# Entering the feed-forward layer: norms on VectorE alone, four gated products between the two halves, weight loads in quarters

## The chip, the cores and the metric

The kernel runs on one NeuronCore of a Trainium2 chip. The engines named below are TensorE (PE, with its weight loads as PEld), VectorE (DVE), ScalarE (ACT), GpSimd (POOL) and SyncE (SP), whose queue issues all DMA transfers of this kernel. Each engine works through its own instructions in a fixed order and waits where an operand or a buffer isn't there yet. The metric is the device time of one execution in microseconds (us).

## The reference

A decoder trunk of two layers, in float32, on 1024 tokens of width 1024. In both layers a mixer is followed by a projection, and that by a gated feed-forward layer (SwiGLU) of width 2816. The part that the change touches, cut from the reference:

```python
def rms_norm(x, g):
    y = x * lax.rsqrt(jnp.mean(x * x, axis=-1, keepdims=True) + EPS)
    return y * g
...
    mixed = jnp.concatenate([y, m_out], axis=-1) @ w_out[l]
    h = h + rms_norm(mixed, norm_mix_post[l])
    gu = rms_norm(h, norm_ffn_pre[l]) @ w_in          # 1024 x 5632
    g, u = gu[..., :D_FF], gu[..., D_FF:]
    f = (jax.nn.silu(g) * u) @ w_out_ffn
    h = h + rms_norm(f, norm_ffn_post[l])
```

Between the projection (`mixed`) and the feed-forward layer stand two norms, one after the other: the first of the projection's output, the second of the sum with the residual.

## The kernel before

Activations lie transposed: eight tiles of 128 features x 512 tokens for each half of the tokens (`H` = 512), held in float32. Each float32 operand of a matmul is split into a high part of type float32r and a low part that is the rest. `split` (L86) makes the high part with a copy on ScalarE (L87) and the low one with a subtraction on VectorE (L88). A product takes three matmuls: high by low, high by high, low by high. Names ending in h and l (`wh`, `wl`, `ah`, `al`, `ch`, `cl`, `th`, `tl`) are such parts; `ah` and `al` are those of the activations.

**The projection** (`mix_half`, L474) makes eight blocks of 24 matmuls (`mm<-al,wh`, L147 to L149) for each half. Layer 0 loads each block's weights (512 KB) for each half anew and splits them: the subtraction is on GpSimd in the first half and on VectorE in the second. In layer 1 the halves lie split in DRAM (`parted`), and `fetch` loads both (`wh` and `wl`, 512 KB each).

**The two norms** (`finish` in `mix_out`, L492). The sum of squares over the features is made with ones as the weights of a matmul (`rcol`, the `oo<-ones,...` rows of L227); `rcp` or `rcn` gets its scale and epsilon on VectorE (L231) and its power -1/2 on GpSimd (L232); a matmul with the identity spreads it over the partitions (`spread`, `oo<-ident,...` of L239), and ScalarE copies that to `rsp` for the first norm and `rsn` (or a tile tagged `hd`) for the second. `post` (L519) multiplies by `rsp` (L524, five of eight tiles on GpSimd), then multiplies by the gain and adds the residual (L526, VectorE), and stores the sum (`hx`). `sums` (L205) adds up the squares for the second norm on two tiles, one for each engine (L217). `scaled` (L534) multiplies by gain and `rsn`: four tiles in one instruction on VectorE (L540), four (`POOL_COPIES`) with a copy on ScalarE (L531) and a product on GpSimd (L538). Then each tile is split into `ah` and `al`.

**The order at the entry.** The first half's norms are worked through during the second half's projection. The second half's norms stand behind that projection. Meanwhile PE works on the first half of feed-forward blocks 0 and 1 (`ffn_plain`, L564: 96 matmuls of L574 to L576), and after these the same blocks for the second half, another 96. The order on each engine is set when the kernel is built, by a scheduler that goes by priorities (`WEIGHT_LEAD`, `EVICT_LEAD`, `NORM_LEAD`) and a simulated time line. `place` (L721) forces the four groups of matmuls of the second half's norms (two `rcol`, two `spread`) in between: the group of index i stands before the plain matmul whose number is `F_PLACES[i]`.

**The other 20 blocks** of 128 of the 2816 hidden features are made in pairs with seven products instead of eight (`ffn_block`, L624): sums and differences of quarters of the weight blocks (`combos`, L600) and of the activations (L742 to L747), 12 matmuls a product (L595 to L597), in the order 1, 5, 6, 2, 7, 3, 4. For each block SP loads the gate's and the up-projection's weights (`wraw`, 512 KB each, three buffers). GpSimd makes the sum `x` of two quarters of the second load (L613) and the other differences (L616, L618, L620), ScalarE and VectorE split them into `ch` and `cl`. Products 1 and 2 need no sums, and only the first half's activations. `out_weights` (L650) loads the output weights (`wo`), combines them and stores them (`wz`) for the last phase; `hidden_combos` stores the hidden features (`xz`).

## Time and profile before

| | |
|---|---|
| median of 3 runs | 2121.84 us (2115.52 to 2125.18) |
| profiled execution | 2116.97 us, of which the span is 2115.1 us |
| mean granted clock of TensorE | 0.974 |
| busy: TensorE, VectorE, ScalarE, GpSimd | 1999.0, 1444.4, 1042.2, 648.9 us |
| layer 0: second half's projection, then entry | 314.6 to 364.5 us, then to 446.2 us |
| layer 1: second half's projection, then entry | 1365.0 to 1405.8 us, from 1419.2 to 1498.2 us |

The span runs from the first to the last instruction of the profiled execution; 1.9 us of its time lie outside. In groups and timelines an instruction is named by its line, engine and operation, then output and inputs by the program's names with shapes, then how many; `[10.19 <-DVE al L88]` means that the engine was idle for 10.19 us before and that VectorE's instruction of line 88, which made `al`, ended that. Matmuls overlap, so PE's pace is read from one start to the next and not from the duration of one.

### The profile page before, as it was taken

The numbers are of one execution on the slowest core, as the hardware profiler recorded it, in microseconds if no ns is written. First come the engines' busy times: TensorE is split into PE (matmuls) and PEld (weight loads), VectorE is DVE, ScalarE is ACT, GpSimd is POOL, SyncE is SP. The second block draws the span as 40 slices with busy tenths as digits, with TensorE's granted clock in tenths as the row PEclk, the third lists the DMA queues.
The fourth block names the chain that finished last, engine by engine and source line by source line (L and its number), as shares of the span: only waits on it lengthen the run. The fifth ranks groups of instructions, "written<-read, shape, count | busy, mean of one in ns | idle before, by whom it ended". The sixth has DMA issues, their size and how long they took to land.

```text
span 2115.1 us, 27580 instructions
## 1 busy us (share of the span) xinstructions
PE 1999.0 (95%) x9400; PEld 1650.8 (78%) x9400; DVE 1444.4 (68%) x2218; ACT 1042.2 (49%) x1977; POOL 648.9 (31%) x575
## 2 busy tenths in 40 slices
PE   7999998799999999999999999887999999999997
PEld 6787776588877787888788878766888888878876
DVE  7877758777767667455878776777765665664566
ACT  6767775344443444444545576643433333344541
POOL 4333543723443431000035431346232233210012
PEclk9999999899999999999999999988999999999998
DMA  5422226137667679666545314152345444485653
GB/s 168 153 80 83 87 80 219 50 122 250 228 225 249 245 255 351 229 207 192 185 177 189 123 58 158 63 197 80 117 157 179 141 159 158 172 285 191 214 176 138
DMA packets 156766, 359.08 MB, mean 170 GB/s; under 512 B 17232, under 2 KB 22608, under 8 KB 156624
## 3 DMA queue, kind: packets, MB, share of 16 engines
q1 hardware_dynamic: 156624, 357.31, 49.2%
q8 instruction: 74, 1.21, 0.2%
q14 instruction: 68, 0.56, 0.1%
HBM read 255.53 MB, written 101.71 MB: 169 GB/s over the span
## 4 chain that ended last, share of the span: by engine, by line
PE 68%; DVE 12%; issue 8%; ACT 6%; POOL 4%; DMA 2%; SPq 0%; DVEq 0%; POOLq 0%; ACTq 0%
PE mm L595 10%; PE mm L597 10%; PE mm L596 9%; PE mm L697 6%; PE mm L698 6%; PE mm L699 6%; PE mm L149 4%; PE mm L147 4%; PE mm L148 4%; DVE acc L526 1%; PE mm L574 1%; PE mm L576 1%; PE mm L575 1%; DVE cl L88 1%; PE oo L1049 1%
## 5 line engine op out<-in xcount | busy, mean ns | idle before, releaser
L87 ACT CAST ch<-wraw 128x512 fp32r<-128x512 f32 x323 | 200.0, 621 | 389.7 <-PE mm L596 199.5
L88 DVE TENSOR_TENSOR cl<-wraw,ch 128x512 fp32r<-128x512 f32 x323 | 234.6, 727 | 188.9 <-ACT ch L87 186.2
L147 PE MATMUL mm<-al,wh 128*128 128x512 f32 x616 | 249.5, 405 | 13.4 <-DVE al L921 8.1
L149 PE MATMUL mm<-ah,wl 128*128 128x512 f32 x616 | 247.9, 403 | 7.0 <-DVE wl L88 5.0
L595 PE MATMUL mm<-al,ch 128*128 128x512 f32 x640 | 252.5, 395 | 1.5 <-DVE c L630 0.8
L597 PE MATMUL mm<-ah,cl 128*128 128x512 f32 x640 | 250.1, 395 | 3.5 <-DVE cl L88 3.5
L596 PE MATMUL mm<-ah,ch 128*128 128x512 f32 x640 | 250.6, 392 | 0.0
L148 PE MATMUL mm<-ah,wh 128*128 128x512 f32 x616 | 246.6, 400 | 0.0
L697 PE MATMUL mm<-tl,ch 128*128 128x512 f32 x532 | 208.1, 391 | 2.2 <-ACT ah L789 2.2
L699 PE MATMUL mm<-th,cl 128*128 128x512 f32 x532 | 206.8, 393 | 1.9 <-DVE cl L88 1.9
L698 PE MATMUL mm<-th,ch 128*128 128x512 f32 x532 | 207.7, 390 | 0.0
L595 PE MATMUL mm<-tl,ch 128*128 128x512 f32 x480 | 189.4, 395 | 1.7 <-ACT c L634 1.6
L596 PE MATMUL mm<-th,ch 128*128 128x512 f32 x480 | 187.8, 391 | 0.0
L597 PE MATMUL mm<-th,cl 128*128 128x512 f32 x480 | 185.4, 391 | 0.0
L613 POOL TENSOR_TENSOR x<-wraw 128x512 f32<-128x512 f32 x40 | 53.1, 1328 | 385.4 <-DMA wraw<-in_wi_dram 374.6
L147 PEld LDWEIGHTS mm<-al,wh 128*128 128x128 f32 x616 | 118.0, 192 | 41.6 <-DVE al L921 10.1
L597 PEld LDWEIGHTS mm<-ah,cl 128*128 128x128 f32 x640 | 120.4, 188 | 34.6 <-DVE cl L88 7.4
L149 PEld LDWEIGHTS mm<-ah,wl 128*128 128x128 f32 x616 | 118.1, 192 | 35.5 <-DVE wl L88 8.1
L595 PEld LDWEIGHTS mm<-al,ch 128*128 128x128 f32 x640 | 120.5, 188 | 28.4 <-ACT ch L87 1.9
L596 PEld LDWEIGHTS mm<-ah,ch 128*128 128x128 f32 x640 | 120.4, 188 | 27.2
L148 PEld LDWEIGHTS mm<-ah,wh 128*128 128x128 f32 x616 | 118.2, 192 | 23.1
L232 POOL TENSOR_TENSOR rcp<-rcp,mhalf 128x4 f32<-128x4 f32 x7 | 7.5, 1072 | 406.8 <-DVE rcp L231 406.8
(349 smaller groups left out, 4602.9 us busy)
## 6 DMA issues: line engine op xcount, KB each, us to landing
wraw<-in_wi_dram SPq DMA_DIRECT2D x88, 512.0 KB, 5.9
xz<-hd SPq DMA_DIRECT2D x154, 256.0 KB, 4.3
th<-xz SPq DMA_DIRECT2D x154, 256.0 KB, 3.5
wo<-in_wf_dram SPq DMA_DIRECT2D x44, 512.0 KB, 5.5
wz<-wo SPq DMA_DIRECT2D x44, 512.0 KB, 3.2
wraw<-wz SPq DMA_DIRECT2D x56, 256.0 KB, 3.3
wraw<-in_wa_dram SPq DMA_DIRECT2D x27, 512.0 KB, 3.5
wraw<-in_wf_dram SPq DMA_DIRECT2D x42, 256.0 KB, 3.5
```

The costliest lines, as they stand in the source:

```text
L87: self.nc.scalar.copy(hi, src)
L88: return (eng or self.nc.vector).tensor_tensor(lo, src, hi.bitcast(F32), op=ALU.subtract)
L147: self.mms += [nc.tensor.matmul(out, wh, al, start=i == 0, stop=False), nc.tensor.matmul(out, wh, ah, start=False, stop=False), nc.tensor. ...
L148: nc.tensor.matmul(out, wh, ah, start=False, stop=False),
L149: nc.tensor.matmul(out, wl, ah, start=False, stop=i == len(ks) - 1)]
L595: ins += [mm(out, wh, xl, start=start and k == 0, stop=False, skip_group_check=not start), mm(out, wh, xh, start=False, stop=False, skip_g ...
L596: mm(out, wh, xh, start=False, stop=False, skip_group_check=not start),
L597: mm(out, wl, xh, start=False, stop=k == 3, skip_group_check=not start)]
L613: ins = nc.gpsimd.tensor_tensor(x, a21, a22, op=ALU.add)
L697: ins += [mm(ps[m], wh[:, m], xl[:, cs], start=start and p == 0, stop=False, skip_group_check=not start), mm(ps[m], wh[:, m], xh[:, cs], s ...
L698: mm(ps[m], wh[:, m], xh[:, cs], start=False, stop=False, skip_group_check=not start),
L699: mm(ps[m], wl[:, m], xh[:, cs], start=False, stop=p == NFB // 2 - 1, skip_group_check=not start)]
```

## The change

1. **Norms on VectorE alone.** `post`, `sums` and `scaled` no longer give instructions to GpSimd; the sum has one tile, the copies on ScalarE (L531) are gone. GpSimd keeps the power, now L237. The sums of the activations (L742 to L747) move to VectorE as well (L755).
2. **Four products between the halves.** Products 1 and 2 of blocks 2 and 3, 48 matmuls, now stand between the first half's 96 plain matmuls and the second half's. Their weight sums are made on VectorE. `F_PLACES` puts the second norm's sum and spread before the matmuls 104 and 116 of that longer list.
3. **Layer 0's projection weights.** The first half splits them on VectorE and stores both parts (`keep`, 16 stores of 512 KB); the second half fetches them.
4. **Quarters.** The feed-forward weights come in pieces of 256 KB: rings of six (`wq`) and four (`wp`) buffers of 256 KB instead of three (`wraw`) and two (`wo`) of 512 KB. SP issues 200 transfers more. `out_weights` does the same, and its first call stands later by one block.

```diff
-A_PLACES, F_PLACES, END_PLACES = (36, 54), (14, 30, 88, 92), (30, 48)
+A_PLACES, F_PLACES, END_PLACES = (36, 54), (14, 30, 104, 116), (30, 48)
-POOL_COPIES = (1, 3, 5, 7)
+OPEN_LEAD = 150
+    def keep(self, key, w):
+        self.parted[key] = self.dp.tile([2, P, D], F32, name=f"kept_{key[0]}{key[1]}")
+        for x, d in zip(w, self.parted[key]):
+            self.nc.sync.dma_start(d.rearrange("p (k c) -> p k c", k=x.shape[1]), x.bitcast(F32))
...
         for m in ms:
-            w = self.fetch(("wo", m)) if layer else self.weight(self.a["wo"][layer, m],
-                                                                eng=self.nc.vector if n else self.nc.gpsimd)
+            if layer or n:
+                w = self.fetch(("wo", m))
+            else:
+                w = self.weight(self.a["wo"][layer, m])
+                self.keep(("wo", m), w)
...
-                      hx, G_FFN_PRE + 8 * layer, self.sums(tiles, "01010111"))
+                      hx, self.sums([(self.nc.vector, total)], "00000000"))
...
-            eng = nc.gpsimd if k % 3 else nc.vector
-            eng.tensor_tensor(x, x, rs, op=ALU.mult)
+            nc.vector.tensor_tensor(x, x, rs, op=ALU.mult)
...
     def scaled(self, f, rs, gain):
         for k in range(KT):
-            if k in POOL_COPIES:
-                self.nc.gpsimd.tensor_tensor(f[k], f[k], rs, op=ALU.mult)
...
+            self.nc.vector.scalar_tensor_tensor(f[k], f[k], self.col(gain + k), rs, op0=ALU.mult, op1=ALU.mult)
...
+    def quads(self, tag, *srcs):
+        tiles = []
+        for src in srcs:
+            for i in range(2):
+                tiles.append(self.t(tag, (P, 4, P)))
+                self.nc.sync.dma_start(tiles[-1], src[:, 4 * i:4 * i + 4])
+        return tiles
...
+    def gated(self, layer, b, xs, order=(1, 5, 6, 2, 7, 3, 4), ring="wq", eng=None, lead=WEIGHT_LEAD):
+        eng = eng or nc.gpsimd
+            a11, a12, a21, a22 = self.quads(ring, *(self.a["wi"][layer, u * NFB + b] for u in range(2)))
...
+        for i in order:
+            with self.tc.high_priority(offset=WEIGHT_LEAD if i in (1, 2) else lead):
+                src = source(i)
+                w = self.t("ch", (P, 4, P), F32R), self.t("cl", (P, 4, P), F32R)
+                self.split(*w, src)
...
+            mms = self.product(ps, w, xs[i], start=not chained)
+            with self.tc.high_priority(offset=EVICT_LEAD):
+                ins = evict(ps)
+            yield mms
...
-        finish([(f"t{h}2{k}",) for h in "hl" for k in range(4)], ("c7", "x"), "hd")
+        finish([(f"t{h}2{k}",) for h in "hl" for k in range(4)], "x", "hd")
+        xs = {1: act[0][0:4], 2: act[0][4:8]}
+        opening = [self.gated(layer, b, xs, (1, 2, 6, 5, 7, 3, 4), ring, nc.vector, OPEN_LEAD)
+                   for b, ring in ((2, "wq"), (3, "wp"))]
+        between = [ins for g in opening for _ in range(2) for ins in next(g)]
         hid[1], mms[1] = self.ffn_plain(ws, act[1])
-        self.place(mms[0] + mms[1], marks, F_PLACES)
+        self.place(mms[0] + between + mms[1], marks, F_PLACES)
...
-            nc.gpsimd.tensor_tensor(x11[k], x12[k], x11[k], op=ALU.subtract)
-            nc.gpsimd.tensor_tensor(x12[k], x22[k], x12[k], op=ALU.subtract)
+            sub(x11[k], x12[k], x11[k])
+            sub(x12[k], x22[k], x12[k])
...
-        ffn = ({"mm": 7, "oo": 1}, dict(ch=4, cl=4), dict(c1=1, c6=1, c7=1, hd=7),
-               dict(x=1, wraw=3, wo=2), quad(2), quad(3), quad(1))
+        ffn = ({"mm": 7, "oo": 1}, dict(ch=4, cl=4), dict(c1=2, c6=1, c7=1, hd=7),
+               dict(x=1, wq=6, wp=4), quad(2), quad(3), quad(1))
```

**Where instructions stand now.** First PE in layer 0, from the second norm's spread (`rcn1`) to the second half's first plain matmul; L574 to L576 of before are L578 to L580 of the change. Before:

```order
L239 MATMUL oo_733_3560<-ident_71,rcn1_731_3556 128x128 x4
L576 MATMUL mm_714_3381<-ah_650_3067,tl31_703_3350 128x512
L574 MATMUL mm_715_3382<-al_651_3068,th33_706_3353 128x512
L575 MATMUL mm_715_3382<-ah_650_3067,th33_706_3353 128x512
L576 MATMUL mm_715_3382<-ah_650_3067,tl33_707_3354 128x512
L574 MATMUL mm_750_3606<-al_735_3568,th10_692_3339 128x512
```

and in the change, where each product of 12 (`mm_754`, `mm_761`, `mm_765`) is shown by its first and last rows:

```order
L244 MATMUL oo_727_3560<-ident_71,rcn1_725_3556 128x128 x4
L601 MATMUL mm_754_3637<-ah_645_3074,cl_753_3634 128x512
L601 MATMUL mm_754_3637<-ah_647_3079,cl_753_3634 128x512
L599 MATMUL mm_761_3664<-al_634_3045,ch_759_3660 128x512
L601 MATMUL mm_761_3664<-ah_639_3059,cl_760_3661 128x512
L599 MATMUL mm_765_3683<-al_642_3065,ch_763_3679 128x512
L601 MATMUL mm_765_3683<-ah_647_3079,cl_764_3680 128x512
L578 MATMUL mm_766_3698<-al_729_3568,th10_683_3339 128x512
```

Four matmuls stood between the spread and the second half; now 28 do, all of first-half activations.

Then VectorE at the same place, from the second norm's scale (`rcn1`) to the first `al` of the second half. Before, with half of the norm's products on GpSimd:

```order
L231 TENSOR_SCALAR rcn1_731_3556<-oo_730_3547 128x4
L88 TENSOR_TENSOR cl_772_3790<-x_768_3782,ch_771_3789 128x512
L586 TENSOR_TENSOR hd_719_3484<-mm_715_3382,c1_718_3483 128x512
L540 SCALAR_TENSOR_TENSOR acc_611_2894<-acc_611_2894,cst_69,hd_732_3559 128x512
L540 SCALAR_TENSOR_TENSOR acc_680_3246<-acc_680_3246,cst_69,hd_732_3559 128x512
L88 TENSOR_TENSOR cl_776_3799<-wraw_766_3778,ch_775_3798 128x512
L88 TENSOR_TENSOR al_735_3568<-acc_611_2894,ah_734_3567 128x512
```

and in the change (of the eight L540 the first and the last are shown):

```order
L236 TENSOR_SCALAR rcn1_725_3556<-oo_724_3551 128x4
L619 TENSOR_TENSOR x_782_3870<-wq_746_3610,wq_747_3612 128x512
L624 TENSOR_TENSOR wq_745_3608<-wq_745_3608,wq_744_3606 128x512
L540 SCALAR_TENSOR_TENSOR acc_610_2916<-acc_610_2916,cst_69,hd_726_3559 128x512
L610 TENSOR_TENSOR c1_751_3631<-c1_751_3631,mm_754_3637 128x512
L540 SCALAR_TENSOR_TENSOR acc_677_3282<-acc_677_3282,cst_69,hd_726_3559 128x512
L88 TENSOR_TENSOR cl_787_3893<-x_782_3870,ch_786_3892 128x512
L755 TENSOR_TENSOR acc_547_2579<-acc_610_2916,acc_547_2579 128x512
L755 TENSOR_TENSOR acc_552_2616<-acc_614_2948,acc_552_2616 128x512
L88 TENSOR_TENSOR al_729_3568<-acc_610_2916,ah_728_3567 128x512
```

All eight products by `rsn` (tile `hd_726`) now stand ahead of the first `al`, with an eviction and two of the activations' sums among them.

Last SP in a steady block pair of layer 1, from the store of the output weights' sums to the load of the block's up-projection weights. Before:

```order
L662 DMA wz1_13746<-wo_3350_16014 128x1024
L662 DMA wz1_13746<-wo_3351_16015 128x1024
L654 DMA wo_3405_16316<-in_wf_dram 128x1024
L666 DMA xz1_1_13739<-hd_3345_15915 128x512
L654 DMA wo_3406_16317<-in_wf_dram 128x1024
L604 DMA wraw_3381_16178<-in_wi_dram 128x1024
```

and in the change:

```order
L672 DMA wz1_13976<-wp_3330_15622 128x512
L553 DMA wp_3391_15938<-in_wf_dram 128x512
L553 DMA wq_3366_15799<-in_wi_dram 128x512
L672 DMA wz1_13976<-wp_3332_15626 128x512
L553 DMA wp_3392_15940<-in_wf_dram 128x512
L553 DMA wp_3393_15942<-in_wf_dram 128x512
L553 DMA wq_3367_15801<-in_wi_dram 128x512
```

The two quarters of the up-projection (`wq_3366`, `wq_3367`) stand behind stores and loads of the output weights, as the single load did before.

More of the change, by code (lines that the diff above doesn't have):

```diff
@@ L54, in __init__ @@
         self.stack = None
[L55 removed]
+        self.marks, self.mms, self.parted = [], [], {}
     def phase(self, name, psum, *pools):
@@ L517, in part, with post @@
         return src[k * P:k * P + P, n * H + cs.start:n * H + cs.stop]
-    def post(self, f, rs, n, gpost, resid, spill, gain=None, take=None, cs=slice(0, H)):
+    def post(self, f, rs, n, gpost, resid, spill, take=None, cs=slice(0, H)):
         nc = self.nc
@@ L527, in post @@
             nc.sync.dma_start(self.part(spill, k, n, cs), x)
-            if gain:
+            if take:
                 take(k, x, r)
-        for k in POOL_COPIES if gain else ():
-            ins = nc.scalar.activation(f[k][:, cs], f[k][:, cs], AF.Copy, scale=self.col(gain + k))
-            self.after(ins, self.square)
     def scaled(self, f, rs, gain):
@@ L555, in ffn_first @@
                 with self.tc.high_priority(offset=WEIGHT_LEAD):
-                    raw = self.t("wraw", (P, KT, P))
-                    self.nc.sync.dma_start(raw, self.a["wi"][layer, u * NFB + b])
-                    for i in range(2):
+                    for i, raw in enumerate(self.quads("wq", self.a["wi"][layer, u * NFB + b])):
                         w = [self.quad(x) for x in tiles[b][2 * u + i]]
-                        self.split(*w, raw[:, 4 * i:4 * i + 4])
+                        self.split(*w, raw)
                         ws[b].append(w)
@@ new lines, in source @@
+        def source(i):
+            if i in (5, 6) and 5 not in made:
+                made[5] = self.t("x", (P, 4, P))
+                eng.tensor_tensor(made[5], a21, a22, op=ALU.add)
+                eng.tensor_tensor(a21, a11, a21, op=ALU.subtract)
+            if i == 6:
+                eng.tensor_tensor(a11, made[5], a11, op=ALU.subtract)
+            if i == 3:
+                eng.tensor_tensor(a12, a12, a11, op=ALU.subtract)
+            return {1: a11, 2: a12, 3: a12, 4: a22, 5: made.get(5), 6: a11, 7: a21}[i]
@@ new lines, in copy, with gate @@
+        def copy(i, ps):
+            part[i] = self.t({1: "c1", 5: "c7", 6: "c6"}[i])
+            return nc.scalar.copy(part[i], ps)
+        def gate(i, ps):
+            add(part[i], part[i], ps)
+            return nc.scalar.activation(part[i], part[i], AF.Silu)
+        steps = {1: (0, lambda ps: copy(1, ps)),
+                 5: (1, lambda ps: copy(5, ps)),
+                 6: (0, lambda ps: copy(6, ps)),
+                 2: (2, lambda ps: gate(1, ps)),
+                 7: (0, lambda ps: add(part[5], part[5], ps)),
+                 3: (1, lambda ps: (gate(6, ps), mul(1, part[6], part[5]))),
+                 4: (0, lambda ps: mul(0, part[1], ps))}
@@ L647, in ffn_block, with finished @@
                     self.evicted = ins
-        return h0, h1
+            yield mms
+        self.hid = hid[0], hid[1]
+    def finished(self, block):
+        for _ in block:
+            pass
+        return self.hid
     def out_weights(self, layer, p):
         nc = self.nc
-        r, s = (self.t("wo", (P, KT, P)) for _ in range(2))
-        for i, d in enumerate((r, s)):
-            nc.sync.dma_start(d, self.a["wf"][layer, 2 * p + i])
-        a11, a21, a12, a22 = r[:, 0:4], r[:, 4:8], s[:, 0:4], s[:, 4:8]
+        a11, a21, a12, a22 = parts = self.quads("wp", *(self.a["wf"][layer, 2 * p + i] for i in range(2)))
         first = nc.vector.tensor_tensor(a22, a21, a22, op=ALU.add)
@@ L766, in ffn @@
         for p in range(1, half):
-            even = self.ffn_block(layer, 2 * p, xs)
+            even = self.finished(opening[0] if p == 1 else self.gated(layer, 2 * p, xs))
             if p == 1:
                 self.hidden_combos(0, hid[0][0], hid[1][0], hid[0][1], hid[1][1])
-            self.out_weights(layer, p if p == half - 1 else p - 1)
+            if p > 1:
+                self.out_weights(layer, p if p == half - 1 else p - 1)
             ahead(2)
-            odd = self.ffn_block(layer, 2 * p + 1, xs)
-            if p == half - 2:
-                self.out_weights(layer, p)
+            odd = self.finished(opening[1] if p == 1 else self.gated(layer, 2 * p + 1, xs))
+            if p in (1, half - 2):
+                self.out_weights(layer, p if p > 1 else 0)
             self.hidden_combos(p, *even, *odd)
```

79 lines of the change are left out of this document (21 added, 58 removed).

## The prediction

> **What bounds the kernel now.** I began with the page, to see which engine sets the end, and whether its clock is held.
>
> ```profile
> span 2115.1 us, 27580 instructions
> PE 1999.0 (95%) x9400; PEld 1650.8 (78%) x9400; DVE 1444.4 (68%) x2218; ACT 1042.2 (49%) x1977; POOL 648.9 (31%) x575
> PEclk9999999899999999999999999988999999999998
> ```
>
> PE is busy 95% of the span, and both kernels run the same products, so the change can only remove PE's gaps, or make new ones. A slice is 52.9 us, and the clock stands at 8 in four of them: the eighth (370 to 423 us), two from 1375 to 1481, and the last. The first three are the entries into the two feed-forward layers. So I cut out those stages. The columns are the window, its length, busy time of PE, PEld, DVE, ACT and POOL with their counts, granted clock, DMA share and GB/s.
>
> ```profile
> 314.60:364.50 49.90, 39.76 (x185) 30.85 (x183) 43.42 (x47) 29.25 (x49) 19.08 (x12) 0.97 0.64 232
> 364.50:446.20 81.70, 66.89 (x280) 54.84 (x281) 61.72 (x66) 31.16 (x54) 40.45 (x26) 0.85 0.12 43
> 1365.00:1405.80 40.80, 38.69 (x177) 32.00 (x177) 26.81 (x27) 17.95 (x31) 18.56 (x13) 0.92 0.82 296
> 1405.80:1419.20 13.40, 4.97 (x26) 4.46 (x25) 8.73 (x14) 5.35 (x10) 2.64 (x2) 0.64 0.07 23
> 1419.20:1498.20 79.00, 66.87 (x266) 54.15 (x266) 64.12 (x70) 33.65 (x59) 40.62 (x24) 0.85 0.20 67
> 1510.00:1870.00 360.00, 358.99 (x1562) 292.41 (x1561) 214.19 (x305) 132.65 (x225) 106.96 (x72) 1.00 0.48 167
> ```
>
> The last row is the steady state: 360.0 us for 1562 matmuls, 0.230 us each, with nothing to win. Rows 1 and 3 are the second half's output projection, rows 2 and 5 the entry: from the first feed-forward matmul to the end of its 192 plain matmuls and 48 of block 2. 240 matmuls at 0.230 are 55.2 us; the rows have 81.7 and 79.0. The waits of PE in those two stretches (layer 0, then layer 1):
>
> ```profile
> PE mm L574 <- DVE al L88: 10.2, 1, 10.2
> PE mm L574 <- ACT acc L480: 5.1, 1, 5.1
> PE oo L227 <- DVE x L217: 2.5, 1, 2.5
> PE oo L227 <- DVE s L203: 2.1, 1, 2.1
> PE oo L227 <- POOL c L217: 2.0, 1, 2.0
> PE mm L149 <- DVE wl L88: 1.8, 3, 0.8
> PE mm L147 <- ACT wh L87: 1.1, 2, 0.7
> ...
> PE mm L574 <- DVE al L88: 8.7, 1, 8.7
> PE oo L227 <- ACT sq L485: 5.2, 1, 5.2
> PE oo L227 <- POOL c L217: 3.3, 1, 3.3
> PE oo L239 <- POOL rcp L232: 1.7, 1, 1.7
> PE oo L227 <- DVE rsn L217: 1.6, 1, 1.6
> ```
>
> The long one, `L574 <- al`, is the second half's activation: PE has run out of first-half work while the second norm is still being applied. After each wait the clock is low too:
>
> ```profile
> 410.56 0.79 PE L574 MATMUL mm<-al,th 128*128 128x512 f32 x1 [10.19 <-DVE al L88]
> 411.58 0.63 PE L576 MATMUL mm<-ah,tl 128*128 128x512 f32 x1
> 415.42 0.63 PE L576 MATMUL mm<-ah,tl 128*128 128x512 f32 x1
> ```
>
> From 411.58 to 415.42 nine matmuls start 0.427 us apart, and twelve in all do: a long wait costs a further 12 x 0.2 = 2.4 us. A page of the Trainium skill, "TensorE: Matmul & The Clock Gate" (What's actually happening), has half rate only after an idle window of some 3.4 us; by it the shorter waits that I keep below (3.0 us) might cost no clock, and the sum would be some 3 us better.
>
> **The change, part by part.** Why is the norm late? Its VectorE and GpSimd rows in layer 0:
>
> ```profile
> 375.92 4.09 DVE L524 TENSOR_TENSOR acc<-acc,rsp 128x512 f32<-128x512 f32 x3 [5.13 <-ACT rsp L243]
> 379.93 5.20 DVE L526 SCALAR_TENSOR_TENSOR acc<-acc,cst,th 128x512 f32<-128x512 f32 x3
> 385.72 0.74 DVE L526 SCALAR_TENSOR_TENSOR acc<-acc,cst,th 128x512 f32<-128x512 f32 x1
> 386.39 0.74 DVE L526 SCALAR_TENSOR_TENSOR acc<-acc,cst,tl 128x512 f32<-128x512 f32 x1
> 408.76 3.42 DVE L88 TENSOR_TENSOR al<-acc,ah 128x512 fp32r<-128x512 f32 x2
> 361.38 3.09 DVE L88 TENSOR_TENSOR al<-acc,ah 128x512 fp32r<-128x512 f32 x5
> 375.96 8.62 POOL L524 TENSOR_TENSOR acc<-acc,rsp 128x512 f32<-128x512 f32 x5 [4.08 <-ACT rsp L243]
> ```
>
> Beside GpSimd a VectorE instruction takes 1.4 to 1.7 us (5.20 / 3, 3.42 / 2), and GpSimd's own as long (8.62 / 5); alone it takes 0.62 (3.09 / 5, the subtraction) or 0.67 (385.72 to 386.39). So two engines together are no faster than VectorE alone: eight products shared took 8.6 us, and alone are 8 x 0.62 = 5.0. Taking GpSimd out of the norm costs VectorE nothing, as long as GpSimd stays idle meanwhile.
>
> *Second norm and second half, layer 0 (81.7 us).* What is left beside 55.2: the sums and spreads on PE, some 40 small ones, 3 us; half clock at the stage's start, 1.8, as now. VectorE's way from `rsp` to the finished sum is 8 x 0.62 + 8 x 0.67 + 15 x 0.62 + a few evictions and weight splits, some 21 us. The sum's matmul now stands at place 104, 24 us behind the start plus those 4.8, while `rsp` comes 11.4 us after the start (375.9 - 364.5): I keep a wait of 0.7. Behind the spread, PE has 28 matmuls of blocks 2 and 3, 6.4 us. In that time VectorE has 8 multiplications at L540 (5.4), one eviction, one `cl`, two x-combinations (L755) and the first `al`, five at 0.6: 8.4 us, and the copy ahead of them 0.9. So `al` is 3.0 us late, with 1.6 us of low clock behind it. Sum 55.2 + 3.0 + 1.8 + 0.7 + 3.0 + 1.6 = 65.3, gain **16.4**. The four weight combinations (L619 to L624) lie ahead of the spread's copy, in the time of the reciprocal. If VectorE kept its contended 1.45, those thirteen would take 18.9 instead of 8.4 and the wait would be that of before: bound 0 for the gain.
>
> *The same in layer 1 (79.0).* The 8.7 and 3.3 go; the same rest, with the low clock of its start, gives 63.5: gain **15.5**.
>
> *Second-half projection, layer 0 (49.9).* Its weights were loaded and split; now they are fetched as halves. The waits on wl and wh, 2.9 us, go; two fetches of 512 KB in 5.5 us of matmuls (24 x 0.230) come instead. Layer 1 does that already:
>
> ```profile
> wh<-parted_wo SPq DMA_DIRECT2D x2, 512.0 KB, 5.3
> wl<-parted_wo SPq DMA_DIRECT2D x2, 512.0 KB, 6.0
> PE mm L149 <- DMA wl<-parted_wo: 0.3, 1, 0.3
> wraw<-in_wi_dram SPq DMA_DIRECT2D x88, 512.0 KB, 5.9
> wo<-in_wf_dram SPq DMA_DIRECT2D x24, 256.0 KB, 3.5
> ```
>
> (The first two are of the window 1378 to 1400, beside its norm's stores, the last two of the whole run.) They need 5.3 and 6.0 us there, as long as the block, and PE waited 0.3. Layer 0 moves more in that time (its residual loads as well), so I take 2 us (bounds 0, and 1 us for each of seven blocks). The 16 new stores leave during the first half, before this window. Ahead of the first feed-forward matmul 2.1 + 5.1 us were lost; in the new order the last block's square still stands behind ScalarE's casts and GpSimd no longer slows the first norm: I keep 2.9. Gain 2.9 + 7.2 - 2 - 2.9 = 5.2, and 1 us of clock (0.97 of 49.9 us is 1.5 lost): **6**.
>
> *Projection and start, layer 1 (40.8 and 13.4).* The 1.6 goes with its low clock, 0.92 of 40.8 us being 3.3 lost: 3.2. Of the 13.4, `rcp` on VectorE now stands behind eight L540 and an `al`, 6 us, which takes the place of 5.2 + 1.7 + 1.5: 10.9 remain, gain 2.5. Together **5.7**.
>
> *Steady blocks.* Four loads of 256 KB in place of two of 512, and 200 more issues on SP, 4 per block among 11. The load that PE waits for is the second pair:
>
> ```profile
> 1713.44 1.29 POOL L613 TENSOR_TENSOR x<-wraw 128x512 f32<-128x512 f32 x1 [10.45 <-DMA wraw<-in_wi_dram]
> 1715.42 1.24 DVE L88 TENSOR_TENSOR cl<-x,ch 128x512 fp32r<-128x512 f32 x1 [3.41 <-ACT ch L87]
> 1717.12 0.39 PE L597 MATMUL mm<-th,cl 128*128 128x512 f32 x1
> ```
>
> GpSimd starts as the load lands, `cl` ends at 1716.66, and PE uses it at once: the slack is under 1 us. A quarter lands in 3.5 us instead of 5.9, so it should be 2 us better, even with a second issue behind it. I take 0: bounds 6 us better (half of the little that the layer-0 blocks lose) and the rival below. "DMA: Bandwidth & Descriptors" in the Trainium skill (Measured) asks for 1 MiB or more per transfer and gives about 2.0 us fixed to each; by its formula, an estimate, a pair of quarters one after the other is 5.2 us against 3.2 for one load, so it speaks against this change, where the rows speak for it (3.5 against 5.9).
>
> **Sum.** 16.4 + 15.5 + 6 + 5.7 = 43.6. The profiled execution was 2116.97 us (span 2115.1 and 1.9 around it), so 2073.4; the median of the runs is 2121.84, 4.9 higher. I predict 2075 for the median, between 2073.4 and 2078.3.
>
> **The rivals.**
> *VectorE becomes the bound of the entry.* All the norm, the combinations and the evictions of four blocks now stand on one in-order engine. For: it was busy 61.7 of 81.7 us; each 0.1 us on some 100 instructions in each entry is 10 us. Against: those 61.7 are contended times, and GpSimd is nearly empty there now. With 0.1 us more per instruction in both layers: about 2093. It also stands for the case that the long wait merely moves.
> *The fetches become the wait in layer 0.* For: 5.3 and 6.0 against a block of 5.5. At 2 us in each of seven blocks instead of 2 in all, with the clock: 12 to 14 us, 2088.
> *Late quarters, the side of slower.* SP issues in order, and the second pair's quarters (L553) stand behind `wp` loads that wait for the wz stores, with no slack. If they come delta late in each of 36 blocks (18 in each layer), the price is 36 x delta: from 1.2 us the gain is gone; at 2 us, 2117 - 43.6 + 72 = 2145. Against: the same loads stood behind `wo` loads before, and quarters land sooner.
> *More than I count.* Quarters give the layer-0 blocks slack and the 2.9 and 3.0 waits vanish: 12 us more, 2061.
>
> **How the numbers follow.** Forecast (2062 to 2084) 0.48; VectorE 0.17; fetches 0.12; late quarters 0.12; more 0.11. Within 0.5% of before (10.6 us, about what a measurement of this kernel can tell from no change) lies the half of the late case with delta near 1.2, 0.06; the other half is slower. So faster 0.88, same 0.06, slower 0.06. The range reaches over both middle rivals and most of the last one, and leaves out the late case and the ends, under 2 in 10: 2052 to 2100.
>
> **What would show it.** After: `al` waits near 3 us instead of 10.2 and 8.7; VectorE's L524/L540 rows at 0.6 to 0.7; no wl/wh waits of the projection on ACT or DVE; entry windows of 65 and 63 us for 240 matmuls. I am wrong if the steady 360 us take over 370, if `al` still waits 6 us or more, or if the projection in layer 0 waits for DMA more than 5.

## The result

The changed kernel takes 2059.39 us (median of 4 runs, 2056.54 to 2060.28) against 2120.26 us (4 runs, 2115.52 to 2125.18): a ratio of 0.971, 95% interval 0.9685 to 0.9736. The forecast was 2075, in a range of 2052 to 2100. The page of the profiled execution:

```profile
span 2057.5 us, 27844 instructions
PE 1976.0 (96%) x9368; PEld 1639.0 (80%) x9368; DVE 1411.4 (69%) x2313; ACT 1022.5 (50%) x1953; POOL 483.7 (24%) x476
PEclk9999999999999999999999999989999999999998
```

The slice at 370 us is back at clock 9; of the two near 1400 us one is left at 8. GpSimd lost 165 us of busy time, and VectorE, which took over its work, lost 33 as well. The stages (columns as in the prediction): layer 0's entry and its 20 blocks; then layer 1's projection (second half), the start of its feed-forward layer, its entry.

```profile
356.70:421.90 65.20, 60.13 (x266) 48.78 (x266) 59.92 (x99) 28.17 (x50) 5.22 (x2) 0.97 0.22 78
421.90:798.30 376.40, 375.15 (x1634) 306.31 (x1633) 265.44 (x366) 159.14 (x279) 134.94 (x96) 1.00 0.74 255
1329.70:1367.10 37.40, 35.53 (x164) 29.33 (x164) 20.57 (x33) 14.15 (x25) 2.03 (x2) 0.95 0.79 285
1367.10:1383.80 16.70, 4.74 (x33) 4.43 (x33) 12.08 (x20) 8.19 (x14) 6.80 (x1) 0.65 0.37 131
1383.80:1446.40 62.60, 59.74 (x258) 48.60 (x258) 57.11 (x93) 30.46 (x55) 1.43 (x1) 0.96 0.23 77
```

The entry of layer 0 took 65.2 us for its 240 matmuls, where 81.7 stood before and 65.3 was forecast; VectorE did 99 instructions in 59.92 us there, 33 more than before in less time. The fourth row is the one that went the other way: 16.70 us where 13.4 stood before. PE's waits, layer 0 and then layer 1:

```profile
PE mm L578 <- DVE al L88: 2.7, 1, 2.7
PE oo L232 <- ACT sq L493: 2.0, 1, 2.0
PE oo L244 <- POOL rcp L237: 1.5, 1, 1.5
...
PE mm L147 <- DMA wh<-kept_wo: 0.6, 1, 0.6
PE mm L149 <- DMA wl<-kept_wo: 0.5, 1, 0.5
...
PE oo L244 <- POOL rcp L237: 11.0, 1, 11.0
PE mm L578 <- DVE al L88: 2.7, 1, 2.7
```

The waits of 10.2 and 8.7 us for `al` are 2.7 each. A new one of 11.0 us, for the power that GpSimd makes, stands in layer 1.

To see where the time went beyond these, I numbered the large matmuls in order of start (7644 in either kernel) and compared the starts of the same number. How much sooner the changed kernel is, with its spans by stage; the last columns are those of the experiments below, each from one profiled execution. The first stage holds the first half's projection and half of the second half's. Kernels whose program is the same there still range from 318.5 (al second) to 322.5 us (no products between), so a few us in one cell mean nothing.

| stage (matmuls) | before | changed | sooner at its end | whole loads | no products between | shared norms | no kept weights | guard | al first | al second |
|---|---|---|---|---|---|---|---|---|---|---|
| up to there (0 to 960) | 320.4 | 320.5 | -0.4 | 319.0 | 322.5 | 325.4 | 321.8 | 320.3 | 321.9 | 318.5 |
| projection and start, layer 0 (to 1056) | 37.5 | 29.2 | 7.9 | 27.9 | 29.2 | 39.8 | 34.2 | 29.7 | 26.1 | 29.2 |
| entry, layer 0 (to 1296) | 81.7 | 65.2 | 24.3 | 69.4 | 77.0 | 70.7 | 63.1 | 64.3 | 64.4 | 60.6 |
| blocks, layer 0 (to 2928) | 385.7 | 376.4 | 33.6 | 388.0 | 376.4 | 375.2 | 375.5 | 378.8 | 377.0 | 377.2 |
| output, layer 0 (to 3852) | 216.4 | 215.8 | 34.2 | 216.0 | 215.8 | 215.8 | 215.8 | 215.8 | 215.8 | 215.8 |
| layer 1 to its start (to 4716) | 370.9 | 369.7 | 35.4 | 368.7 | 370.6 | 368.9 | 369.4 | 367.3 | 370.4 | 368.0 |
| entry, layer 1 (to 4956) | 79.0 | 62.6 | 51.7 | 62.2 | 70.5 | 63.9 | 63.0 | 65.3 | 63.7 | 59.2 |
| blocks, layer 1 (to 6576) | 374.0 | 372.9 | 52.9 | 372.9 | 372.9 | 372.9 | 372.9 | 375.4 | 373.8 | 373.7 |
| output, layer 1 (to 7643) | 226.2 | 224.4 | 54.6 | 224.2 | 222.7 | 228.3 | 224.2 | 224.8 | 224.7 | 223.3 |

The span ends 57.6 us sooner. The two entries gave 16.5 and 16.4, as forecast (16.4 and 15.5). What was not forecast: 9.3 us from layer 0's blocks, and 4.7 at the very end (1.7 up to the last matmul, 3.0 behind it); and of the 5.7 forecast for layer 1's projection and start next to nothing came. By the forecast's own windows these took 40.8 + 13.4 us before and take 37.4 + 16.7 now; the table's row, which begins with layer 1, has 1.2.

### The profile page after: what moved, and what is told of

Its sections match the earlier page's. It is cut to its first block, busy times and chain, and to the rows that moved or that the text cites. A ratio compares the mean times of both kernels' runs of the same rounds, so it can differ in the third digit from the quotient of the medians.

```text
span 2057.5 us, 27844 instructions
## 1 busy us (share of the span) xinstructions
PE 1976.0 (96%) x9368; PEld 1639.0 (80%) x9368; DVE 1411.4 (69%) x2313; ACT 1022.5 (50%) x1953; POOL 483.7 (24%) x476
## 4 chain that ended last, share of the span: by engine, by line
PE 79%; DVE 8%; ACT 4%; DMA 3%; issue 3%; POOL 2%; SPq 0%; POOLq 0%; DVEq 0%; ACTq 0%
PE mm L599 12%; PE mm L601 12%; PE mm L600 12%; PE mm L707 6%; PE mm L708 6%; PE mm L709 6%; PE mm L149 5%; PE mm L147 4%; PE mm L148 4%; PE mm L578 1%; PE mm L579 1%; PE mm L580 1%; PE oo L1064 1%; DVE acc L540 1%; DVE al L88 1%
## 5 line engine op out<-in xcount | busy, mean ns | idle before, releaser
L87 ACT CAST ch<-wq 128x512 fp32r<-128x512 f32 x311 | 193.3, 621 | 437.9 <-PE mm L600 229.2
L88 DVE TENSOR_TENSOR cl<-wq,ch 128x512 fp32r<-128x512 f32 x311 | 234.2, 754 | 193.6 <-ACT ch L87 118.8
L610 DVE TENSOR_TENSOR c<-c,mm 128x512 f32<-128x512 f32 x120 | 82.4, 686 | 114.3 <-PE mm L601 114.2
L619 POOL TENSOR_TENSOR x<-wq,wq 128x512 f32<-128x512 f32 x36 | 49.1, 1364 | 338.6 <-DMA wq<-in_wi_dram 246.9
```

Source lines behind the costliest of these rows:

```text
L87: self.nc.scalar.copy(hi, src)
L88: return (eng or self.nc.vector).tensor_tensor(lo, src, hi.bitcast(F32), op=ALU.subtract)
L610: add = lambda o, x, y: nc.vector.tensor_tensor(o, x, y, op=ALU.add)
```

## The experiments

### Each part undone

**The quarters.** The changed kernel with whole loads, and the kernel before with quarters alone:

```diff
-            for i in range(2):
-                tiles.append(self.t(tag, (P, 4, P)))
-                self.nc.sync.dma_start(tiles[-1], src[:, 4 * i:4 * i + 4])
+            whole = self.t(tag, (P, KT, P))
+            self.nc.sync.dma_start(whole, src)
+            tiles += [whole[:, 0:4], whole[:, 4:8]]
...
-               dict(x=1, wq=6, wp=4), quad(2), quad(3), quad(1))
+               dict(x=1, wq=3, wp=2), quad(2), quad(3), quad(1))
```

> The changed kernel, with its feed-forward weights again loaded in pieces of 512 KB (three and two buffers of 512 KB, stores of the output weights' sums in 512 KB too); all else as changed. The changed kernel has 2059.4 us. Theory A: the 9 us that layer 0's steady blocks gained (matmul 1260 of the run came 24.3 us sooner than before, matmul 2928 33.6 us) come from the quarters, since GpSimd's sum of the second pair no longer waits for 512 KB: 2068 to 2071, and those 9 us are lost between 420 and 800 us. Rival B: they come from something else in the change (the moved products, GpSimd's freed time), and 200 more transfers cost or bring nothing: 2057 to 2062.

> The kernel before with nothing but the quarters (rings of six and four buffers of 256 KB, all feed-forward weight loads and the stores of the output weights' sums in 256 KB). The kernel before has 2120.3 us. Theory A: the steady blocks of layer 0 gain the same 9 us, the entries nothing: 2109 to 2113. Rival B: within 3 us of before. Rival C (late quarters, the side of slower of the prediction): over 2130.

Measured: 2070.85 us with whole loads (ratio to before 0.9764, 0.9745 to 0.9784), and 2108.82 for before with quarters (0.9942, 0.9924 to 0.9961). Of the 200 transfers that the change adds, 176 are the quarters'; the other 24 come from the kept weights. Theory A holds from both sides: 11.5 us lost by the one, 12.2 gained by the other. In the table the loss stands in layer 0's blocks: 388.0 against 376.4. In the trace of before with quarters the same blocks take 379.2 us instead of 385.7, 6.5 of the 9 that theory A had there, and layer 1's entry, where it had nothing, takes 74.8 instead of 79.0; the two profiled executions are 7.5 us apart. The waits of GpSimd for the second load in that stage (us in total, times, longest), and the time from issue to landing, in before and then in the changed kernel (window 446 to 798 us for its landings):

```profile
POOL x L613 <- DMA wraw<-in_wi_dram: 189.8, 19, 22.2
wraw<-in_wi_dram SPq DMA_DIRECT2D x35, 512.0 KB, 6.2
```
```profile
POOL x L619 <- DMA wq<-in_wi_dram: 129.6, 17, 9.1
wq<-in_wi_dram SPq DMA_DIRECT2D x66, 256.0 KB, 5.2
```

PE's waits from 446 to 800 us, first in before, then with whole loads; in the changed kernel none of these is left:

```profile
PE mm L597 <- DVE cl L88: 2.9, 4, 2.2
PE mm L595 <- ACT ch L87: 0.7, 2, 0.4
```
```profile
PE mm L600 <- ACT ch L87: 3.5, 3, 1.7
PE mm L602 <- DVE cl L88: 3.3, 5, 1.4
```

These waits are only a part of the loss. From one start of a large matmul to the next, before has 36 distances over 0.3 us in these blocks, which together cost 10.9 us above the usual 0.23 each; whole loads have 34 (12.9 us), the changed kernel 2 (1.5 us).

A quarter lands only 1.0 us sooner in this crowded stage (DMA share 0.74), and GpSimd's sum `x` reads both quarters of the second load, so it starts when the later one has landed. Most of the gain is an earlier issue. In the traces, over blocks 5 to 21 of layer 0 (medians), whole loads issue the second load 9.3 us ahead of the block's first matmul, and it lands 3.3 us ahead of it; in the changed kernel the later quarter is issued 11.6 us ahead and lands 6.2 us ahead. Of the 2.9 us, 2.3 come from the earlier issue and 0.6 from the shorter landing. That the issue is earlier because a ring of quarters comes free piece by piece is argued: no run changed the ring without the size of the transfer.

In layer 1's blocks, where the DMA share is about 0.5, the kernels with and without quarters take the same 372.9 us. The rule of the Trainium skill, "DMA: Bandwidth & Descriptors" (Measured), to put 1 MiB or more in a transfer, pointed the other way here: it is stated for the share of the peak bandwidth, and what counted here was the moment at which two given pieces had landed.

**The products between the halves.**

```diff
-        between = [ins for g in opening for _ in range(2) for ins in next(g)]
...
-        self.place(mms[0] + between + mms[1], marks, F_PLACES)
+        self.place(mms[0] + mms[1], marks, F_PLACES)
```

> The changed kernel without the four products between the halves: products 1 and 2 of blocks 2 and 3 stand with their blocks again (with the changed order of products, their sums on VectorE), and the second norm's sum and spread go before the plain matmuls 88 and 92 as before. Theory A: the products are cover for VectorE's norm; 48 matmuls of 0.23 us are 11 us of cover in each layer, less some 3 us that VectorE saves ahead of the first activation: the waits of PE at the second half grow by 8 to 9 us a layer, 2075 to 2079. Rival B: VectorE is the bound and the products only move the wait: under 2064.

Measured: 2076.21 us (0.979, 0.9769 to 0.9812), 16.8 more than the changed kernel. The entries are 77.0 and 70.5 us instead of 65.2 and 62.6, and the waits are as before:

```profile
PE mm L578 <- DVE al L88: 9.2, 1, 9.2
...
PE mm L578 <- DVE al L88: 9.4, 1, 9.4
```

Theory A holds. VectorE's norm takes what it takes; the products only give PE something to do meanwhile.

**The norms.** VectorE and GpSimd share them again, with ScalarE's copies, the sum on two tiles and before's early place of the first `al` (only the activations' sums of L755 stay on VectorE). From the edit:

```diff
-            nc.vector.tensor_tensor(x, x, rs, op=ALU.mult)
+            eng = nc.gpsimd if k % 3 else nc.vector
+            eng.tensor_tensor(x, x, rs, op=ALU.mult)
...
+            if k in POOL_COPIES:
+                self.nc.gpsimd.tensor_tensor(f[k], f[k], rs, op=ALU.mult)
```

> The changed kernel with the norms shared between VectorE and GpSimd (and the copies on ScalarE) as before; the products between the halves, quarters and kept weights stay. Theory A: two engines together are no faster than VectorE alone, 8.6 us against 5.0 for eight products by the rows of before; some 7 us in each exposed second norm, and the 4 to 5 us that the run's last norms gained: 2074 to 2080. Rival B: the order and the cover made the gain, the sharing costs nothing: 2058 to 2064.

Measured: 2086.02 us (0.9842, 0.9824 to 0.9861), 26.6 more than the changed kernel: the largest of the parts, and more than either theory had. First the eight products by `rsp` of the second half in layer 0 with two engines, then the changed kernel's products and gains on VectorE alone:

```profile
383.71 4.09 DVE L532 TENSOR_TENSOR acc<-acc,rsp 128x512 f32<-128x512 f32 x3 [6.50 <-ACT rsp L249]
383.75 8.61 POOL L532 TENSOR_TENSOR acc<-acc,rsp 128x512 f32<-128x512 f32 x5 [5.46 <-ACT rsp L249]
```
```profile
367.61 4.91 DVE L530 TENSOR_TENSOR acc<-acc,rsp 128x512 f32<-128x512 f32 x8 [2.74 <-ACT rsp L248]
372.44 2.73 DVE L532 SCALAR_TENSOR_TENSOR acc<-acc,cst,th 128x512 f32<-128x512 f32 x4
375.09 2.73 DVE L532 SCALAR_TENSOR_TENSOR acc<-acc,cst,tl 128x512 f32<-128x512 f32 x4
```

Products and gains together took VectorE 10.2 us, where with two engines the products alone took 8.6. By the table the rest of the loss stands in layer 0's projection and start, 39.8 us against 29.2, where I had expected none. There the first half's norm is worked through, and PE waits for it and for the weights:

```profile
PE mm L148 <- DMA wh<-kept_wo: 6.1, 2, 4.6
PE oo L233 <- DVE s L209: 5.0, 1, 5.0
```

The fetches stand among the `hx` stores in SP's order, and those wait for the slower norm; that this is why `wh` comes late is argued from the order, not shown by a run. The kept weights, which gain little by themselves, may even lose here: no run shared the norms without them.

**The kept weights of layer 0.**

```diff
-            if layer or n:
-                w = self.fetch(("wo", m))
-            else:
-                w = self.weight(self.a["wo"][layer, m])
-                self.keep(("wo", m), w)
+            w = self.fetch(("wo", m)) if layer else self.weight(self.a["wo"][layer, m],
+                                                                eng=self.nc.vector if n else self.nc.gpsimd)
```

> The changed kernel without the kept projection weights of layer 0: loaded and split for both halves as before, the low part on GpSimd in the first half and on VectorE in the second. Theory A: the second half's projection loses again what the fetches brought, waits on wl and wh of some 3 us, and VectorE carries six subtractions more ahead of the first norm: 2062 to 2066. Rival B: the fetches brought nothing (in the changed kernel PE waits 1.05 us for them too): 2058 to 2061.

Measured: 2062.21 us (0.973, 0.9714 to 0.9746). It is 2.8 more than the changed kernel, but the two intervals overlap, so theory A is only the likelier. The trace has the projection and start at 34.2 us instead of 29.2, and 2 of these 5 us come back in the entry. The waits on `wl` and `wh` that theory A named aren't there: from 300 us to the entry PE waits 3.9 us for the first half's `rsn` and 3.7 for an `al`, so the likelier cause is VectorE's added subtractions, which come ahead of the norm.

The four parts undone one by one cost 11.5 + 16.8 + 26.6 + 2.8 = 57.7 us of the 60.9: they nearly add up, so each is worth about that in this kernel; the 2.8 may be noise.

### The wait of 11.0 us

In layer 1, VectorE and GpSimd in the changed kernel, from the second norm factor of the first half to the power of the second half's first norm:

```profile
1369.11 5.39 DVE L540 SCALAR_TENSOR_TENSOR acc<-acc,cst,rsn 128x512 f32<-128x512 f32 x8 [6.16 <-DMA wp<-in_wi_dram]
1375.02 0.16 DVE L236 TENSOR_SCALAR rcp<-oo 128x4 f32<-128x4 f32 x1
1375.09 4.30 DVE L88 TENSOR_TENSOR al<-acc,ah 128x512 fp32r<-128x512 f32 x7
1379.30 1.89 DVE L88 TENSOR_TENSOR tl<-wq,th 128x512 fp32r<-128x512 f32 x3
1375.25 6.80 POOL L237 TENSOR_TENSOR rcp<-rcp,mhalf 128x4 f32<-128x4 f32 x1 [12.04 <-DVE rcp L236]
```

The 6 us of `rcp` behind eight L540 and an `al` were forecast. The power was not: 512 numbers, whose median time is 1.02 us, took 6.80 (in layer 0 3.80), and ended 0.9 us after VectorE's row of ten subtractions. To test whether VectorE keeps GpSimd out, `guard` makes VectorE wait for the power:

```diff
             rc = self.rcol(s, tag, w)
+            if guard:
+                held, rc = rc, self.tile(self.sp, 1, f"rg{tag}", (P, 4), F32)
+                self.guard = self.nc.vector.tensor_copy(rc, held)
...
+        self.after(self.lows[1], self.guard)
```

> The changed kernel, in which VectorE waits for GpSimd's power of the second half's first norm: behind the row that makes rcp it copies the power's result (128x4), and the spread reads that copy, so VectorE stands still while GpSimd works. In the changed kernel that power took 3.80 us in layer 0 and 6.80 us in layer 1, instead of 1.02, and ended some 0.9 us after VectorE's last subtraction in a row. Theory A: VectorE's back-to-back work keeps GpSimd out: the power takes 1.0 to 1.1 us in both layers, rsp comes 2 us earlier in layer 0 and 5 in layer 1, and PE's wait of 11.0 us in layer 1 falls to 6: 2052 to 2057. Rival B: the duration is no effect of VectorE (a rough span, a slow start of GpSimd): the power stays over 3 us and the time within 2 us of 2059.

Its power and PE's wait in layer 1:

```profile
1380.57 1.01 POOL L237 TENSOR_TENSOR rcp<-rcp,mhalf 128x4 f32<-128x4 f32 x1 [12.12 <-DVE rcp L236]
PE oo L244 <- DVE rgp L256: 5.5, 1, 5.5
```

So the mechanism of theory A holds: with VectorE standing still the power takes 1.01 us (1.41 in layer 0), and the wait halves. From the projection's last matmul to the end of layer 1's entry it is 76.7 us instead of 79.6. But the kernel as a whole takes 2062.76 us (0.9726, 0.9711 to 0.974), no gain, where theory A had 2052 to 2057; the last section shows what ate it.

The same by itself, behind the end of the changed kernel (for each kind such a group; `vec` is the row of twelve):

```diff
+            rc, ins = ready(i)
+            self.after(ins, last)
+            prev = ins
+            pool(rc)
+            for j in range(12 if vec else 0):
+                x = vec(j)
+                self.after(x, prev)
+                prev = x
+            last = close(i, rc, ins, prev)
```

> The changed kernel with a measurement behind its last norm: a small GpSimd instruction (128x4) started while VectorE runs twelve instructions of 128x512 in a row: power alone (L930), power beside subtractions into float32r (L931), beside scalar_tensor_tensor (L932), beside products in float32 (L933), beside tensor_scalar with one tensor input (L934), an addition 128x4 beside subtractions (L935), an addition of 128x512 beside subtractions (L938). Its time is longer by these rows and says nothing else. Theory A: instructions of VectorE with two tensor inputs that follow one another without a gap keep GpSimd from its operands: L931 to L933 and L935 take 7 to 9 us (until the row of twelve ends), L930 and L934 1.0. Rival B: only the subtractions into float32r do it: L931 long, L932 and L933 1.0 to 1.7. Rival C: it is the power's own start that is slow: L935 short where L931 is long. For L938, theory A has it as long as the row of twelve as well; from the shared norms of before (1.6 to 1.7 us for each of both engines) one would expect 1.7.

Alone the power took 1.01 us. Beside rows of twelve it took 1.38 (subtractions), 1.45 (scalar_tensor_tensor), 8.00 (products) and 1.29 (one tensor input), and an addition beside subtractions 7.20; the addition of 128x512 had nothing to wait for, started in the middle of an earlier row and took 1.49. That fits no theory: rival B falls with the products, rival C with the addition, and theory A with the 1.38. So it was repeated:

> The earlier measurement repeated: six times each a power of 128x4 on GpSimd beside twelve VectorE rows of 128x512, in this order: subtractions into float32r (POOL L931), products in float32 (L933), scalar_tensor_tensor (L932), tensor_scalar with one tensor input (L934). The single measurement had 1.38, 8.00, 1.45 and 1.29 us, and 7.20 for an addition beside the subtractions that left the power at 1.38. Theory A: whether GpSimd gets in is settled by the moment at which it asks, not by VectorE's operation: both lengths, near 1.4 and near 8, appear within one or more of the three kinds with two inputs, and never for one input. Rival B: the kind decides: six of one length within each kind.

GpSimd's powers, two of each kind in order (start, duration):

```profile
2057.82 8.00 POOL L931 TENSOR_TENSOR acc<-acc,mhalf 128x4 f32<-128x4 f32 x1 [7.91 <-DVE acc L909]
2066.17 1.38 POOL L931 TENSOR_TENSOR acc<-acc,mhalf 128x4 f32<-128x4 f32 x1 [0.35 <-DVE acc L909]
2104.98 8.00 POOL L933 TENSOR_TENSOR acc<-acc,mhalf 128x4 f32<-128x4 f32 x1 [5.99 <-DVE acc L909]
2113.34 1.38 POOL L933 TENSOR_TENSOR acc<-acc,mhalf 128x4 f32<-128x4 f32 x1 [0.35 <-DVE acc L909]
2152.15 1.44 POOL L932 TENSOR_TENSOR acc<-acc,mhalf 128x4 f32<-128x4 f32 x1 [5.99 <-DVE acc L909]
2200.70 4.80 POOL L934 TENSOR_TENSOR acc<-acc,mhalf 128x4 f32<-128x4 f32 x1 [6.66 <-DVE acc L909]
2205.85 1.29 POOL L934 TENSOR_TENSOR acc<-acc,mhalf 128x4 f32<-128x4 f32 x1 [0.35 <-DVE acc L909]
```

Subtractions and products alternate strictly, 8.00 and 1.38, three times each; tensor_scalar alternates 4.80 and 1.29, and 4.80 is about its whole row; scalar_tensor_tensor let the power through six times out of six in 1.44. So kind and moment both count, and rival B falls as well as A's "never for one input". The short ones follow a pause: VectorE had waited for the long power ahead of them. The long ones follow a row that ran on without one. A reading that fits these: a row of VectorE instructions that is already running without a gap holds GpSimd off until it ends, scalar_tensor_tensor excepted.

A rival that these rows leave is GpSimd's own pause, 0.35 us ahead of the short ones and 2.87 or more ahead of the long ones. The changed kernel's powers in layer 0 speak against it:

```profile
361.95 3.80 POOL L237 TENSOR_TENSOR rcp<-rcp,mhalf 128x4 f32<-128x4 f32 x1 [19.62 <-DVE rcp L236]
385.65 1.42 POOL L237 TENSOR_TENSOR rcn<-rcn,mhalf 128x4 f32<-128x4 f32 x1 [19.90 <-DVE rcn L236]
```

GpSimd stood idle equally long ahead of both, and VectorE worked on beside both. But ahead of the second VectorE had just paused for 1.21 us, and ahead of the first it had run on for 14 us.

The Trainium skill, "SBUF — State Buffer" (SBUF: two separate sides), says that VectorE and GpSimd share a pair of ports by a lock, and that the loser waits for the whole instruction of the winner. The trace agrees that one waits; but it waited for a row of twelve, and not for one instruction.

### The remaining 2.7 us

All eight products by the second norm's factor stand ahead of the first `al`; in before it stood behind two. If the first `al` comes after two of them again, the wait should go:

```diff
-            self.nc.vector.scalar_tensor_tensor(f[k], f[k], self.col(gain + k), rs, op0=ALU.mult, op1=ALU.mult)
+            ins = self.nc.vector.scalar_tensor_tensor(f[k], f[k], self.col(gain + k), rs, op0=ALU.mult, op1=ALU.mult)
+            if k > 1:
+                self.after(ins, lows[k - 2])
...
-            sub(x11[k], x12[k], x11[k])
+            self.after(sub(x11[k], x12[k], x11[k]), lows[-1])
```

> The changed kernel, in which VectorE makes the activation of tile k-2 before it multiplies tile k by the second norm's factor (al between the rows of L540 instead of behind all eight), and the activations' sums (L755) stand behind the last al. Theory A: the first al comes some 5 us sooner, the two waits of 2.69 us at the second half go, with 1.6 us of low clock each: 2050 to 2053. Rival B: VectorE's total work is the bound, and the wait comes back at a later al or at block 2's remaining products: 2057 to 2060.

> al_first and guard together. Theory A: their gains add up, 8 + 5 us: 2044 to 2048. Rival B: both only move VectorE's work about, and the gain is that of the better one: 2050 to 2054.

Measured: 2055.84 us (0.9698, 0.9683 to 0.9713) and, with the guard, 2072.38 (0.9771, 0.9756 to 0.9786): the first lies between its theories, and the second is 13 us slower than the changed kernel, against both theories. The wait for `al` is gone in both. In layer 1, in al first, stands another:

```profile
PE mm L581 <- ACT th L87: 11.0, 2, 9.4
```

These are the high parts of the feed-forward weights. The edit changed the first half's order too; ScalarE's casts of the first half's `ah` then wait for VectorE tile by tile (the last one 5.46 us), and the weights' casts are queued behind them. With the guard in the way the longest such wait was 13.0 us. So the edit was confined to the second half (`if n and k > 1`), without and with the guard:

> As al_first, but the new order of VectorE's rows only for the second half of the tokens; the first half's multiplications and subtractions keep the changed kernel's order. In al_first, layer 0's entry was 4 us shorter than in the changed kernel (matmul 960 to 1296 in 90.6 us instead of 94.4), and layer 1's 3 us longer (matmul 4600 to 5040 in 129.1 instead of 126.0), where PE waited 9.4 us for the weights' high parts (th) on ScalarE. Theory A: those casts stood behind casts of the first half's activations that wait for VectorE's new order; with the first half's order untouched, layer 1 keeps the 11.0 us wait for rcp and loses the 2.69 us one: 2050 to 2053. Rival B: the wait for al only moves to a later row of VectorE: 2057 to 2060.

> al_second with guard's copy behind the power. Theory A: the power is short in both layers, and layer 1's wait for it falls from 11.0 to 5.5 us as in guard, where its entry was 2.3 us shorter (123.7 against 126.0): 2 to 3 us below al_second, 2047 to 2051. Rival B: the copy holds VectorE as long as it frees GpSimd, no gain over al_second within 1.5 us.

Measured: 2049.51 us (0.9668, 0.9655 to 0.9682; 5 runs, 2046.39 to 2051.19) and 2055.3 with the guard (0.9696, 0.9683 to 0.9709). Theory A of the first holds, half a us beyond its range: it beats the changed kernel by 9.9 us, with entries of 60.6 and 59.2 us. What PE waits for in layer 0, and in layer 1:

```profile
PE oo L232 <- ACT sq L493: 2.0, 1, 2.0
...
PE oo L244 <- POOL rcp L237: 11.0, 1, 11.0
```

With the guard the stretch from layer 1's projection to the end of its entry is again shorter (72.6 us against 76.1), so the mechanism of theory A is there, but the kernel is 5.8 us slower, outside both theories. The two profiled executions are 7.5 us apart: 4.7 are lost in the blocks of the two layers, which the last section takes up, and 4.0 in the first stage, ahead of anything that the guard touches; these mean nothing.

## Why the prediction was right, and where it was not

The time is in the range, but not for every reason given. It lies just under the inner forecast (2062 to 2084) and close to the rival "more than I count" (2061, chance 0.11). Of that rival one half came true, the slack that quarters give layer 0's blocks; the waits of 2.9 and 3.0 us did not vanish (2.0 and 2.7).

- **Entries: right, with some luck in layer 0's sum.** 65.3 and 63.5 us were forecast, 65.2 and 62.6 measured. The wait for `al` was 2.69 us where 3.0 stood, with the same queue ahead of it, and the clock loss behind it was the 1.6 us of the forecast: from 399.31 us on seven starts follow at 0.43 us (here the wait and the first of them).

```profile
398.24 0.50 PE L578 MATMUL mm<-al,th 128*128 128x512 f32 x1 [2.69 <-DVE al L88]
399.31 0.63 PE L579 MATMUL mm<-ah,th 128*128 128x512 f32 x1
```

  These came after an idle time of 2.69 us, so the rule of "TensorE: Matmul & The Clock Gate" in the Trainium skill (What's actually happening), by which it takes an idle window of some 3.4 us, would have missed them. Two terms of the sum were off and cancelled: the 1.8 us of low clock at the stage's start wasn't paid, and a wait of 1.5 us for the held-off power stands in no term. The wait of 0.7 us ahead of the second norm's sum doesn't follow from its own figures either: 11.4 + 21 us against 24 + 4.8 leaves 3.6. It measured 0.9, because VectorE's way from `rsp` to the sum took 16.6 us (from 367.61 us to the last L222 at 384.20) and not 21: seven additions instead of fifteen.
- **"Taking GpSimd out of the norm costs VectorE nothing": right, and too modest.** Undoing it costs 26.6 us. I priced it mostly where the second half's norms are exposed; 10.6 of the 26.6 stand ahead of that, in layer 0's projection and start. The step "gain 2.9 + 7.2 - 2 - 2.9" for that stage gave 6 and measured 8.3 (8.8 from the matmul at which the forecast's window begins), although the waits it keeps were near: 2.0 for the square where 2.9 stood, 1.05 for the fetches where 2 stood.
- **Layer 1's start: wrong in sign.** "10.9 remain, gain 2.5": 16.7 remained. The step that failed took the power at its usual 1 us, beside VectorE; it took 6.80. Without that surplus of 5.8 the stage would have been 10.9, and with the guard, where the power took 1.01, it was indeed 5.5 us shorter. The projection ahead of it gave 3.4 us where 3.2 were forecast.
- **Steady blocks: "I take 0" was mis-sized.** They gave 9.3 us in layer 0, beyond the bound of 6. The slack under 1 us was read rightly. The bound took half of what the layer-0 blocks lose, without a reason for the half: their late starts cost 10.9 us before and 1.5 now. The landing time that spoke for the quarters, 3.5 against 5.9, was of the whole run and of other loads: here it is 5.2 against 6.2, and the earlier issue, which the prediction doesn't have, does more. The rival "late quarters" is out: both kernels with quarters gain.
- **The end: left out.** `post` serves the last norms as well. Their products and gains in the second of the last stage's two pieces, first in before, shared between VectorE and GpSimd, then on VectorE alone:

```profile
2105.03 2.15 DVE L524 TENSOR_TENSOR acc<-acc,c 128x256 f32<-128x256 f32 x3 [2.49 <-ACT c L243]
2105.07 4.41 POOL L524 TENSOR_TENSOR acc<-acc,c 128x256 f32<-128x256 f32 x5 [1.76 <-ACT c L243]
2107.11 4.24 DVE L526 SCALAR_TENSOR_TENSOR acc<-acc,cst,hd 128x256 f32<-128x256 f32 x7
```
```profile
2048.06 2.77 DVE L530 TENSOR_TENSOR acc<-acc,c 128x256 f32<-128x256 f32 x8 [1.98 <-ACT c L248]
2050.75 2.85 DVE L532 SCALAR_TENSOR_TENSOR acc<-acc,cst,hd 128x256 f32<-128x256 f32 x7
```

  From the first product to the last gain but one these are 5.5 us instead of 6.3, and about the same in the first piece; where the rest of the 4.7 us lies wasn't followed.

Against the forecast of 43.6 the trace has 57.6: +9.3 and +1.1 for the blocks of the two layers, +4.7 for the end, +2.3 for layer 0's projection and start, +1.0 for the entries, +0.6 for layer 0's output, -4.5 for layer 1 up to its start and -0.4 ahead of it all make 14.1, and 0.1 is rounding. So the range held with 7 us to spare: the misses mostly point one way, and that they stayed within it is partly luck.

## What to carry to other kernels

Before work is shared between VectorE and GpSimd, compare one engine's rate alone with both rates side by side; here two were slower than one, and a tiny GpSimd instruction on the critical path could wait for a whole row of VectorE's. When a norm can't be made shorter, find products that need none of its results and put them in PE's order behind the point where it runs dry. And where a consumer has no slack, ask when the last piece that it needs can be issued and lands, not only what bandwidth the size of the transfer gives.

## What was not expected of the hardware

**GpSimd held off by a row of VectorE instructions**, as shown above: 1.01 us alone, 8.00 beside twelve products in float32 or subtractions in a row that ran on from work ahead of it, 1.38 beside the same rows after a pause of VectorE, 4.80 or 1.29 in the same way beside twelve with one input, 1.44 beside scalar_tensor_tensor. What exactly opens the door is open.

**PE's pace depends on something that the instructions don't show.** From 1520 to 1780 us, in layer 1's blocks, neither kernel of this pair waits for anything, and the matmuls are the same. In these 260 us the changed kernel and then al second with the guard work on so many of them:

```profile
1520.00:1780.00 260.00, 260.00 (x1131) 211.92 (x1130) 158.53 (x218) 95.53 (x162) 76.85 (x55) 1.00 0.49 161
```
```profile
1520.00:1780.00 260.00, 260.00 (x1123) 210.33 (x1122) 155.39 (x216) 94.53 (x160) 75.75 (x54) 1.00 0.47 156
```

That is 0.2299 against 0.2315 us per matmul, 0.7%, at the same granted clock. All three kernels with the guard have the slower pace (their blocks in layer 1 take 375.4 to 376.3 us, those of the table's other kernels with the change 372.9 to 373.8); over the two layers' blocks that is some 5 us, more than the 3 us that the guard gained in layer 1. The guard's one new tile of 128x4 lies ahead of the feed-forward buffers in memory and moves their addresses by 32 bytes. That the addresses are the cause is argued from this: no run moved a tile and did nothing else, and a guard that needs no new tile wasn't tried.
